# More summed pairs in a feed-forward down product: the first group's and the last 1024 columns'

## The chip, the cores and the metric

The kernel runs on one core of one Trainium2 chip. The metric is the device time of one launch in microseconds (us), the median of several runs. The times of the kernel before come from three runs; one further execution was recorded by the hardware profiler, and all rows of the trace are from that one.

## The reference, cut to what matters

One encoder block on 256 tokens of width 2048 in float32. Two attentions side by side, a cross attention and a gated feed-forward each add to the running sum x, and a last RMSNorm closes it:

```python
x = x + concat([mla(h), diff_attn(h)]) @ w_out      # h = rms_norm(x, g_mix), projected by w_in
x = x + cross_attention(rms_norm(x), rms_norm(mem)) @ w_xo
hf = rms_norm(x, g_ffn)
x = x + (silu(hf @ w_gate) * (hf @ w_up)) @ w_down  # w_gate, w_up: 2048 x 5632; w_down: 5632 x 2048
return rms_norm(x, g_final)
```

The change touches the last product, by `w_down`, and the end of it most of all.

## The kernel before

**Products in three parts.** Every float32 operand is split in two fp32r terms: a high one, which ScalarE (ACT) makes by a cast (line 103), and a low one, which VectorE (DVE) makes as the operand minus its high term (line 104). `mm` then issues three matmuls for one product, with lines of their own: 95 (high by high), 96 (high activation by low weight), 97 (low activation by high weight). A weight block thus passes SyncE's (SP) DMA queue into a `wraw` buffer, ACT into `wh`, DVE into `wl`, and TensorE (PE) last. There are three `wraw` buffers and four each of `wh` and `wl`. The two token halves (tt 0 and 1) are 128 rows each; activations are the stationary operand, 128x128, and weights the moving one, 512 or 256 columns wide. Results gather in eight PSUM banks in two sets of four, which swap their parts after each wide product.

**Plain and summed pairs.** Wide products take the contraction in pairs: 256 rows, two blocks of 128, by 1024 columns, two tiles of 512. A plain pair ("P" in a string of kinds) is 2 blocks x 2 token halves x 2 column tiles = 8 products, 24 matmuls of 512, and its weights take two splits of 128x1024. A summed pair ("W") does the same 2x2x2 block product with seven products instead of eight (a Strassen-Winograd scheme), 21 matmuls. Its weights cost sums ahead of the splits: in `wide_project`, one add of 128x1024 (line 726), two of 128x512 (730 and 731) in a single buffer called `tsum`, and then splits of 1024 (`wh`/`wl`, from the raw block), 1024 (from the sums), 512 (raw) and 1024 (from the sums, in buffers `wh2`/`wl2` of which there is one each). Four of the seven products go into banks of their own, Q 1, 5, 6 and 7, which sum over all summed pairs of one wide product; after the last of these, `leave` (lines 777 to 785 in `wide_add`) adds them to the running sum x in eight DVE steps and one ACT copy, and at the end of the product `join` (788) adds the four plain accumulators. The activation side of a summed pair is made once by `summed_pair` (four 128x128 subtractions, lines 689 to 692, and splits).

**The feed-forward in groups.** The 5632 hidden columns are one narrow chunk of 512 and five wide ones of 1024; a chunk's gate and up products, SiLU (842) and multiply (852) are followed by transposes (858), so that each wide chunk yields four pairs for the down product and the narrow one two. Group 0 is the narrow chunk and one wide chunk: six pairs, kinds `PPPPPW`. Groups 1 and 2 have two wide chunks, eight pairs each, kinds `PPWWPPPW`. Each group multiplies its pairs with their rows of `w_down` and adds the result to x, for columns 0 to 1023 and 1024 to 2047 in turn.

**The end.** In group 2, the first half of the columns is a `wide_add` of all eight pairs. As each of its column tiles is joined, `final` squares it on ACT for the norm (line 199) and multiplies it by `g_final` on GpSimd (POOL, line 893). The second half is done in columns of 512: tile 2 by `project`, four pieces of four plain 128-row blocks, 96 matmuls of 512; then tile 3 as four accumulations of 256 columns (two token halves by two column halves), 192 matmuls of 256. There the first ten blocks are multiplied as they come, and the last six are held split in activation buffers, so that the four accumulations end one after another while the norm of the earlier ones is under way.

**What sets the order.** Each engine runs its instructions in an order that a scheduler fixed when the program was built; only the weight loads on SP keep the order of the code. An engine waits at an instruction until its operands and its buffer are there, and everything queued behind it on the engine waits too.

Of the kernel before, what the change touches and what calls it, by code (L numbers as in the profile page):

```python
# [19 lines left out]
P = 128  # L20
S = 256
NT = S // P
D = 2048
# [16 lines left out]

G_ORDER, U_ORDER = (0, 1, 2, 3, 4, 5, 6, 7), (0, 2, 1, 4, 3, 6, 5, 7)

DN_KINDS = "PP" + "PPPW" + ("PPWW" + "PPPW") * (NPC // 2)

PLAIN, SUMS = ((0, 0), (0, 1), (1, 0), (1, 1)), ((0, 1), (0, 0), (1, 1), (1, 0))
EPS = 1e-6
# [30 lines left out]
def encoder_block(ctx: ExitStack, tc: tile.TileContext, a, out):  # L77
# [15 lines left out]
    def mm(o, l, r, start, stop):  # L93

        nc.tensor.matmul(o, l.h, r.h, start=start, stop=False)  # L95
        nc.tensor.matmul(o, l.h, r.l, start=False, stop=False)  # L96
        nc.tensor.matmul(o, l.l, r.h, start=False, stop=stop)  # L97
# [597 lines left out]
        split_into(f[:, 4:8, :], s)  # L695
        return Pair(forms=f)

    def wide_project(pairs, src, order, kinds, leave, join):

        accs = [[acc_tile() for _ in range(2)] for _ in range(NT)]
        used = [[False] * 2 for _ in range(NT)]
        summed = [i for i in order if kinds[i] == "W"]
        Q = {}  # L710
        for n, i in enumerate(order):
            stop = n == len(order) - 1
            raw = pair_raw(src[i])
# [12 lines left out]
            nc.vector.tensor_tensor(out=t[:, 0:2, :], in0=raw[:, 1:3, :],  # L726
                                    in1=raw[:, 0:1, :].to_broadcast([P, 2, 512]), op=ALU.add)
            t13 = split_blocks(t[:, 0:2, :])
            b21 = split_blocks(raw[:, 3:4, :])
            nc.vector.tensor_tensor(out=t[:, 2, :], in0=t[:, 0, :], in1=raw[:, 2, :], op=ALU.add)  # L730
            nc.vector.tensor_tensor(out=t[:, 3, :], in0=t[:, 2, :], in1=raw[:, 3, :], op=ALU.add)  # L731
# [12 lines left out]
        for tt in range(NT):  # L744
            for oc in range(2):
                join(tt, oc, accs[tt][oc])
        banks.reverse()

    def wide_result(pairs, src, order, kinds):

# [15 lines left out]
        wide_project(pairs, src, order, kinds, leave, join)  # L766
        return res

    def wide_add(pairs, src, order, kinds, oc0, done=None):


        def x(tt, oc):
            return x_res[tt][:, (oc0 + oc) * 512:(oc0 + oc + 1) * 512]

        def leave(Q):
            v, u = nat("v"), nat("u")
            nc.scalar.copy(out=u, in_=Q[1])
            nc.vector.tensor_tensor(out=v, in0=Q[6], in1=u, op=ALU.subtract)
            nc.vector.tensor_tensor(out=x(0, 0), in0=x(0, 0), in1=Q[1], op=ALU.add)
            nc.vector.tensor_tensor(out=u, in0=Q[5], in1=v, op=ALU.add)  # L780
            nc.vector.tensor_tensor(out=v, in0=v, in1=Q[7], op=ALU.subtract)
            nc.vector.tensor_tensor(out=x(1, 1), in0=x(1, 1), in1=Q[5], op=ALU.add)
# [9 lines left out]
        wide_project(pairs, src, order, kinds, leave, join)  # L792

    def normalized_pairs():

# [72 lines left out]
    fss = small.tile([P, NT, 7], F32, name="fss", tag="fss", bufs=1)  # L868
    nc.gpsimd.memset(fss[:, :, 4:5], EPS)

    groups = [([0], (0, 1, 2, 5, 3, 4)), ([1, 2], (0, 1, 2, 4, 3, 6, 7, 5)), ([3, 4], (0, 1, 2, 4, 3, 6, 7, 5))]
    pair0 = 0
    for gi, (chunks, order) in enumerate(groups):
        hp = []
# [20 lines left out]
        def xT(kt):  # L895
            return tuple(hp[kt // 2].at(kt % 2, tt) for tt in range(NT))

        wide_add(hp, src[0], order, kinds, 0, final)
        for oc in (2, 3):
            pieces = [a["w_down"][c, oc - 2] for c in range(len(hp) // 2)]  # L900
            if oc == 2:
                add_out(project(xT, pieces), oc)
                for tt in range(NT):
                    final(tt, oc)
                continue

            accs = [(acc_tile(), ps_tile("acc2")) for _ in range(NT)]
            n = 4 * len(pieces) - 6
            kt = 0
            ws = []  # L910

            def last_mm(tt, h, kt, w, stop):
                mm(accs[tt][h][:, :256], xT(kt)[tt], w[:, h * 256:(h + 1) * 256], kt == 0, stop)
# [10 lines left out]
            for tt in range(NT):  # L924
                for h in range(2):
                    for i, w in enumerate(ws):
                        last_mm(tt, h, n + i, w, i == len(ws) - 1)
                    xs = x_res[tt][:, oc * 512 + h * 256:oc * 512 + (h + 1) * 256]
                    nc.vector.tensor_tensor(out=xs, in0=xs, in1=accs[tt][h][:, :256], op=ALU.add)
                    if h == 0:  # L930
                        meansq(xs, fss[:, tt, 3:4], 256, D)
                        nc.vector.tensor_tensor(out=xs, in0=xs, in1=gfb[1][:, 512:768], op=ALU.mult)
                        nc.vector.reduce_sum(out=fss[:, tt, 5:6], in_=fss[:, tt, 0:5], axis=AX.X)
                        continue
                    sq = nat("sq")[:, :256]
                    nc.vector.tensor_tensor_reduce(out=sq, in0=xs, in1=xs, scale=1.0 / D, scalar=fss[:, tt, 5:6],
                                                   op0=ALU.mult, op1=ALU.add, accum_out=fss[:, tt, 6:7])
                rf = small.tile([P, 1], F32, name="rf", tag="rf")
                nc.gpsimd.tensor_tensor(out=rf, in0=fss[:, tt, 6:7], in1=mhalf[:, :1], op=ALU.pow)
                xr, orow = x_res[tt], out[tt * P:(tt + 1) * P, :]  # L940
                nc.vector.tensor_scalar(out=xr[:, :384], in0=xr[:, :384], scalar1=rf, scalar2=None, op0=ALU.mult)
                nc.sync.dma_start(out=orow[:, :384], in_=xr[:, :384])
                nc.scalar.activation(xr[:, 384:1152], xr[:, 384:1152], AF.Copy, scale=rf)
                nc.scalar.dma_start(out=orow[:, 384:1152], in_=xr[:, 384:1152])
                nc.vector.scalar_tensor_tensor(out=xs, in0=xs, scalar=rf, in1=gfb[1][:, 768:1024],
                                               op0=ALU.mult, op1=ALU.mult)
                nc.vector.tensor_scalar(out=xr[:, 1152:1792], in0=xr[:, 1152:1792], scalar1=rf, scalar2=None,
                                        op0=ALU.mult)
                nc.sync.dma_start(out=orow[:, 1152:], in_=xr[:, 1152:])

# [20 lines left out]
def _lay_out(i):  # L971
# [38 lines left out]
        "w_down": _pieces(i["w_down"][0][-2048:, 1024:]).transpose(1, 0, 2, 3, 4),  # L1010
    }
    return {k: np.ascontiguousarray(v) for k, v in arrays.items()}

# [16 lines left out]
```

## Time and profile before

| | us |
|---|---|
| median of three runs (1147.09 to 1147.89) | 1147.54 |
| the profiled execution | 1148.3 |
| its span, first to last instruction | 1146.5 |
| last matmul starts, from the span's start | 1138.94 |
| mean granted TensorE clock | 0.998 |
| VectorE busy | 944.0 |
| ScalarE busy | 633.8 |

The span is what the instructions cover; 1.8 us of the profiled execution lie outside it. The page gives busy time by engine, the chain of work that ended last, and groups of equal instructions by code line; behind it, the trace answers for one engine and a stretch of time. In a row of the timeline stand the start, the length, the engine, the line, the operation and what it reads and writes; numbers of buffers are left out of the names there.

### The profile page before, as it was taken

How to read it: one execution, taken by the hardware profiler on the slowest of the kernel's cores; microseconds unless marked ns; L12 is line 12 of the kernel's file. 1: busy time of each engine (PE TensorE's matmuls, PEld its weight loads, DVE VectorE, ACT ScalarE, POOL GpSimd, SP SyncE). 2: the span in 40 equal slices, each digit the busy share in tenths (PEclk: the TensorE clock that was granted, in tenths of full speed). 3: DMA queues.
4: the chain of work that ended last, by engine and by line, in shares of the span. 5: the costliest groups of instructions: out<-in, count | busy, mean ns of one | idle time of the engine just before them, and what ended most of it. 6: DMA issues, size and time to landing. Idle time of an engine off the chain costs nothing.

```text
span 1146.5 us, 14402 instructions
## 1 busy us (share of the span) xinstructions
PE 1137.0 (99%) x5471; PEld 954.7 (83%) x5471; DVE 944.0 (82%) x1256; ACT 633.8 (55%) x895; POOL 69.4 (6%) x81
## 2 busy tenths in 40 slices
PE   9999999999999999999999999999999999999997
PEld 7888888888888888888888888888888888888887
DVE  6788766686868677989888888998999898998973
ACT  6755454454566555665544555665554564654652
POOL 4920000000000000000000000000000000000021
PEclk9999999999999999999999999999999999999999
DMA  9655334444854444455555556555555555565561
GB/s 343 234 198 184 143 113 181 163 168 164 313 196 172 150 177 166 169 206 197 210 194 196 194 198 220 183 187 217 184 192 212 206 198 198 192 240 210 189 220 75
DMA packets 33766, 222.15 MB, mean 194 GB/s; under 512 B 4128, under 2 KB 4896, under 8 KB 8992
## 3 DMA queue, kind: packets, MB, share of 16 engines
q1 hardware_dynamic: 32256, 216.86, 52.5%
q0 software_dynamic: 864, 3.15, 0.8%
q10 hardware_dynamic: 576, 1.21, 0.3%
q8 instruction: 43, 0.70, 0.2%
q14 instruction: 27, 0.22, 0.1%
HBM read 219.11 MB, written 2.10 MB: 193 GB/s over the span
## 4 chain that ended last, share of the span: by engine, by line
PE 98%; issue 0%; DMA 0%; DVE 0%; ACT 0%; POOLq 0%; POOL 0%; DVEq 0%; ACTq 0%
PE acc L95 27%; PE acc L97 27%; PE acc L96 27%; PE q L97 3%; PE q L96 3%; PE q L95 3%; PE pt L331 2%; PE ppt L478 1%; PE psc L97 1%; PE psc L96 1%; PE psc L95 1%; PE acckv L95 0%; PE acckv L96 0%; PE acckv L97 0%; PE pt L858 0%
## 5 line engine op out<-in xcount | busy, mean ns | idle before, releaser
L103 ACT CAST wh<-wraw 128x1024 fp32r<-128x1024 f32 (+2 forms) x399 | 392.8, 999 | 353.1 <-PE acc L97 301.6
L104 DVE TENSOR_TENSOR wl<-wraw,wh 128x1024 fp32r<-128x1024 f32 (+2 forms) x399 | 459.9, 1165 | 127.8 <-ACT wh L103 125.9
L96 PE MATMUL acc<-wl,x2n_h 128*128 128x512 f32 x320 | 124.5, 390 | 0.0
L97 PE MATMUL acc<-wh,x2n_l 128*128 128x512 f32 x320 | 123.9, 389 | 0.0
L103 ACT CAST wh<-tsum 128x1024 fp32r<-128x1024 f32 x82 | 85.8, 1051 | 43.9 <-DVE tsum L731 15.1
L104 DVE TENSOR_TENSOR wl<-tsum,wh 128x1024 fp32r<-128x1024 f32 x82 | 99.6, 1220 | 12.5 <-ACT wh L103 12.5
L95 PE MATMUL acc<-wh,x2n_h 128*128 128x512 f32 x320 | 108.1, 390 | 0.0
L96 PE MATMUL acc<-wl,x0T_h 128*128 128x512 f32 x224 | 88.3, 395 | 0.0
L97 PE MATMUL acc<-wh,x0T_l 128*128 128x512 f32 x224 | 88.2, 395 | 0.0
L95 PE MATMUL acc<-wh,x0T_h 128*128 128x512 f32 x224 | 87.3, 395 | 0.8 <-ACT x0T_h L106 0.8
L96 PE MATMUL acc<-wl,hT_h 128*128 128x512 f32 (+1 forms) x192 | 73.0, 383 | 0.0
L97 PE MATMUL acc<-wh,hT_l 128*128 128x512 f32 (+1 forms) x192 | 72.1, 381 | 0.0
L97 PEld LDWEIGHTS acc<-wh,x2n_l 128*128 128x128 f32 x320 | 60.1, 188 | 12.4
L96 PEld LDWEIGHTS acc<-wl,x2n_h 128*128 128x128 f32 x320 | 60.1, 188 | 12.3
L95 PEld LDWEIGHTS acc<-wh,x2n_h 128*128 128x128 f32 x320 | 59.9, 188 | 12.2
L95 PE MATMUL acc<-wh,hT_h 128*128 128x512 f32 (+1 forms) x192 | 64.4, 382 | 0.0
L96 PE MATMUL q<-wl,forms_h 128*128 128x512 f32 x164 | 63.8, 389 | 0.0
L97 PE MATMUL q<-wh,forms_l 128*128 128x512 f32 x164 | 63.5, 389 | 0.0
L95 PE MATMUL q<-wh,forms_h 128*128 128x512 f32 x164 | 57.6, 389 | 0.0
L96 PE MATMUL acc<-wl,forms_h 128*128 128x512 f32 (+1 forms) x151 | 57.0, 378 | 0.0
L97 PE MATMUL acc<-wh,forms_l 128*128 128x512 f32 (+1 forms) x151 | 56.9, 378 | 0.0
L95 PE MATMUL acc<-wh,forms_h 128*128 128x512 f32 (+1 forms) x151 | 56.6, 378 | 0.0
(383 smaller groups left out, 2296.8 us busy)
## 6 DMA issues: line engine op xcount, KB each, us to landing
wraw<-in_w_gate SPq DMA_DIRECT2D x44, 1024.0 KB, 4.8
wraw<-in_w_up SPq DMA_DIRECT2D x44, 1024.0 KB, 4.8
wraw<-in_w_dn SPq DMA_DIRECT2D x36, 1024.0 KB, 4.8
wraw<-in_w_in SPq DMA_DIRECT2D x24, 1024.0 KB, 4.8
wraw<-in_w_out SPq DMA_DIRECT2D x16, 1024.0 KB, 4.8
wraw<-in_w_down SPq DMA_DIRECT2D x8, 1024.0 KB, 4.8
wraw<-in_w_in_lat SPq DMA_DIRECT2D x7, 832.0 KB, 7.7
wraw<-in_w_xk SPq DMA_DIRECT2D x4, 1024.0 KB, 5.7
```

The source lines that it names most:

```text
L95: nc.tensor.matmul(o, l.h, r.h, start=start, stop=False)
L96: nc.tensor.matmul(o, l.h, r.l, start=False, stop=False)
L97: nc.tensor.matmul(o, l.l, r.h, start=False, stop=stop)
L103: last_cast[0] = nc.scalar.copy(out=dst.h, in_=src).ins
L104: last_split[0] = nc.vector.tensor_tensor(out=dst.l, in0=src, in1=dst.h.bitcast(F32), op=ALU.subtract).ins
L331: nc.tensor.transpose(out=pt[:, j * P:(j + 1) * P], in_=src[:, j * P:(j + 1) * P], identity=ident)
L478: nc.tensor.transpose(out=pt[:, kt * S + tt * P:kt * S + (tt + 1) * P], in_=p[:, tt, kt * P:(kt + 1) * P], identity=ident)
```

## The change

Three things are changed.

1. In group 0, the fifth pair (index 4) becomes a summed one: kinds `PPPPWW`, in the order 0, 1, 2, 4, 5, 3. This holds for both halves of the columns.
2. In group 2, the second half of the columns starts with a `wide_add` of five pairs, 0, 2, 3, 7, 1 in this order, with kinds P, W, W, W, P. The Q banks are left as ever; of the plain accumulators only column tile 3's are joined (`closed=(1,)`), and those of tile 2 are handed back open.
3. The remaining pairs 4, 5 and 6, all plain, follow by column tile: 36 matmuls of 512 go on in the open accumulators of tile 2, and then 72 of 256 columns do tile 3 from six weight blocks held in activation buffers, again as four accumulations one after another, which are added to x beside what the five joint pairs gave it. Their weights come in six loads of 512 KB (three of each tile); the second half's `w_dn` pairs come in five loads of 1024 KB. Before, the same 8 MB came in eight loads.

The whole program has 5396 matmuls instead of 5471: 4490 of 512 columns instead of 4445, 504 of 256 instead of 624, the others as before.

```diff
-DN_KINDS = "PP" + "PPPW" + ("PPWW" + "PPPW") * (NPC // 2)
+DN_KINDS = "PP" + "PPWW" + ("PPWW" + "PPPW") * (NPC // 2)
...
-    def wide_project(pairs, src, order, kinds, leave, join):
+    def wide_project(pairs, src, order, kinds, leave, join, closed=(0, 1)):
...
-                            mm(accs[tt][oc], pairs[i].at(k, tt), w[k][:, oc, :], not used[tt][oc], stop and k == 1)
+                            mm(accs[tt][oc], pairs[i].at(k, tt), w[k][:, oc, :], not used[tt][oc],
+                               stop and k == 1 and oc in closed)
...
-            for oc in range(2):
+            for oc in closed:
                 join(tt, oc, accs[tt][oc])
         banks.reverse()
+        return accs
...
-    groups = [([0], (0, 1, 2, 5, 3, 4)), ([1, 2], (0, 1, 2, 4, 3, 6, 7, 5)), ([3, 4], (0, 1, 2, 4, 3, 6, 7, 5))]
+    groups = [([0], (0, 1, 2, 4, 5, 3)), ([1, 2], (0, 1, 2, 4, 3, 6, 7, 5)), ([3, 4], (0, 1, 2, 4, 3, 6, 7, 5))]
...
         wide_add(hp, src[0], order, kinds, 0, final)
-        for oc in (2, 3):
-            pieces = [a["w_down"][c, oc - 2] for c in range(len(hp) // 2)]
-            if oc == 2:
-                add_out(project(xT, pieces), oc)
...
-            for p in pieces:
-                for w in weights(p, pool=act_tile if kt + 4 > n else None):
-                    if kt < n:
-                        for tt in range(NT):
-                            for h in range(2):
-                                last_mm(tt, h, kt, w, False)
-                    else:
-                        ws.append(w)
-                    kt += 1
...
+        accs = wide_add(hp, src[1], (0, 2, 3, 7, 1), kinds, 2, closed=(1,))
+        kts = [2 * i + k for i in (4, 5, 6) for k in range(2)]
+        kt = 0
+        for p in range(3):
+            for w in weights(a["w_down"][0, p]):
                 for tt in range(NT):
-                    final(tt, oc)
-                continue
+                    mm(accs[tt][0], xT(kts[kt])[tt], w, False, kt == 5)
+                kt += 1
+        add_out([accs[tt][0] for tt in range(NT)], 2)
+        for tt in range(NT):
+            final(tt, 2)
+
+        ws = [w for p in range(3) for w in weights(a["w_down"][1, p], pool=act_tile)]
+        oc = 3
+        for tt in range(NT):
+            for h in range(2):
+                acc = acc_tile("acc2")[:, :256]
+                for i, w in enumerate(ws):
+                    mm(acc, xT(kts[i])[tt], w[:, h * 256:(h + 1) * 256], i == 0, i == len(ws) - 1)
```

The rest of the end, the norm and the writes of the output, is the same code. By two or three lines, what stands behind the edits has moved down: the adds are lines 728, 732 and 733 now, `leave` 780 to 788, `join` 791.

VectorE's queue of before at the start of the second column half: the first split of the half's weights is row 1 (`wl_9495`), rows with `v`, `u` and `xres` are the first half's `leave` and `join`.

```order
L104 TENSOR_TENSOR wl_9495<-wraw_9492,wh_9494 128x1024
L778 TENSOR_TENSOR v_9429<-q6_9233,u_9430 128x512
L104 TENSOR_TENSOR wl_9499<-wraw_9492,wh_9498 128x1024
L780 TENSOR_TENSOR u_9430<-q5_9231,v_9429 128x512
L782 TENSOR_TENSOR xres1_109<-xres1_109,q5_9231 128x512
L781 TENSOR_TENSOR v_9429<-v_9429,q7_9232 128x512
L783 TENSOR_TENSOR xres0_108<-xres0_108,u_9430 128x512
L788 TENSOR_TENSOR xres0_108<-xres0_108,acc_9156 128x512
L104 TENSOR_TENSOR wl_9529<-wraw_9526,wh_9528 128x1024
```

The same place of the changed program; `tsum_9561` is the second half's first sum, `wraw_9555` the weights it is made of:

```order
L104 TENSOR_TENSOR wl_9524<-wraw_9521,wh_9523 128x1024
L781 TENSOR_TENSOR v_9456<-q6_9260,u_9457 128x512
L104 TENSOR_TENSOR wl_9528<-wraw_9521,wh_9527 128x1024
L728 TENSOR_TENSOR tsum_9561<-wraw_9555 128x1024
L783 TENSOR_TENSOR u_9457<-q5_9258,v_9456 128x512
L785 TENSOR_TENSOR xres1_109<-xres1_109,q5_9258 128x512
L791 TENSOR_TENSOR xres0_108<-xres0_108,acc_9183 128x512
L732 TENSOR_TENSOR tsum_9561<-tsum_9561,wraw_9555 128x512
L104 TENSOR_TENSOR wl_9563<-wraw_9555,wh_9562 128x1024
L784 TENSOR_TENSOR v_9456<-v_9456,q7_9259 128x512
L786 TENSOR_TENSOR xres0_108<-xres0_108,u_9457 128x512
L104 TENSOR_TENSOR wl_9568<-tsum_9561,wh_9567 128x1024
```

The wide add stands right behind the two plain splits now, and the rest of the sum's work among the first half's `leave` and `join`. VectorE's queue goes on with the end of that first sum and the second pair's (`wraw_9602`, `tsum_9604`):

```order
L733 TENSOR_TENSOR tsum_9561<-tsum_9561,wraw_9555 128x512
L787 TENSOR_TENSOR xres1_109<-xres1_109,v_9456 128x512
L788 TENSOR_TENSOR xres1_109<-xres1_109,v_9456 128x512
L791 TENSOR_TENSOR xres0_108<-xres0_108,acc_9184 128x512
L104 TENSOR_TENSOR wl_9572<-wraw_9555,wh_9571 128x512
L791 TENSOR_TENSOR xres1_109<-xres1_109,acc_9185 128x512
L791 TENSOR_TENSOR xres1_109<-xres1_109,acc_9186 128x512
L104 TENSOR_TENSOR wl2_9578<-tsum_9561,wh2_9577 128x1024
L104 TENSOR_TENSOR wl_9606<-wraw_9602,wh_9605 128x1024
L728 TENSOR_TENSOR tsum_9604<-wraw_9602 128x1024
L732 TENSOR_TENSOR tsum_9604<-tsum_9604,wraw_9602 128x512
L733 TENSOR_TENSOR tsum_9604<-tsum_9604,wraw_9602 128x512
```

From `tsum_9561`'s wide add to `tsum_9604`'s, both counted, stand 6 steps of 1024 and 13 of 512. Behind them come splits of 1024 (`wl_9611`), 512 (`wl_9615`), 1024 (`wl_9649`) and 1024 (`wl2_9621`), the third sum's wide add (`tsum_9647`), two half adds and the split `wl_9654`.

TensorE's queue of the changed program where the second sum is used:

```order
L96 MATMUL q1_9557<-wl_9606,forms_h_8473 128x512
L97 MATMUL q1_9557<-wh_9605,forms_l_8474 128x512
L96 MATMUL acc_9518<-wl_9606,forms_h_8473 128x512
L97 MATMUL acc_9518<-wh_9605,forms_l_8474 128x512
L95 MATMUL q5_9558<-wh_9610,forms_h_8473 128x512
L95 MATMUL q7_9559<-wh_9610,forms_h_8473 128x512
L95 MATMUL acc_9517<-wh_9614,forms_h_8473 128x512
L95 MATMUL q1_9557<-wh_9648,forms_h_9164 128x512
L95 MATMUL acc_9518<-wh_9648,forms_h_9164 128x512
L96 MATMUL q5_9558<-wl_9611,forms_h_8473 128x512
```

The fifth of these rows, the first to read a cast of `tsum_9604`, is the 60th matmul from the first of the second half; the first to read `wh_9653`, the third sum's, is the 81st, and the first to read `wl_9654` the 84th.

More of the change, by code (lines that the diff above doesn't have):

```diff
@@ L767, in wide_result, with wide_add @@
         return res
-    def wide_add(pairs, src, order, kinds, oc0, done=None):
+    def wide_add(pairs, src, order, kinds, oc0, done=None, closed=(0, 1)):
         def x(tt, oc):
@@ L790, in join @@
                 done(tt, oc0 + oc)
-        wide_project(pairs, src, order, kinds, leave, join)
+        return wide_project(pairs, src, order, kinds, leave, join, closed)
     def normalized_pairs():
@@ new lines, in encoder_block @@
+        oc = 3
[4 more added lines that the diff above has]
+                    mm(acc, xT(kts[i])[tt], w[:, h * 256:(h + 1) * 256], i == 0, i == len(ws) - 1)
+                xs = x_res[tt][:, oc * 512 + h * 256:oc * 512 + (h + 1) * 256]
+                nc.vector.tensor_tensor(out=xs, in0=xs, in1=acc, op=ALU.add)
+                if h == 0:
+                    meansq(xs, fss[:, tt, 3:4], 256, D)
+                    nc.vector.tensor_tensor(out=xs, in0=xs, in1=gfb[1][:, 512:768], op=ALU.mult)
+                    nc.vector.reduce_sum(out=fss[:, tt, 5:6], in_=fss[:, tt, 0:5], axis=AX.X)
+                    continue
+                sq = nat("sq")[:, :256]
+                nc.vector.tensor_tensor_reduce(out=sq, in0=xs, in1=xs, scale=1.0 / D, scalar=fss[:, tt, 5:6],
+                                               op0=ALU.mult, op1=ALU.add, accum_out=fss[:, tt, 6:7])
+            rf = small.tile([P, 1], F32, name="rf", tag="rf")
+            nc.gpsimd.tensor_tensor(out=rf, in0=fss[:, tt, 6:7], in1=mhalf[:, :1], op=ALU.pow)
+            xr, orow = x_res[tt], out[tt * P:(tt + 1) * P, :]
+            nc.vector.tensor_scalar(out=xr[:, :384], in0=xr[:, :384], scalar1=rf, scalar2=None, op0=ALU.mult)
+            nc.sync.dma_start(out=orow[:, :384], in_=xr[:, :384])
+            nc.scalar.activation(xr[:, 384:1152], xr[:, 384:1152], AF.Copy, scale=rf)
+            nc.scalar.dma_start(out=orow[:, 384:1152], in_=xr[:, 384:1152])
+            nc.vector.scalar_tensor_tensor(out=xs, in0=xs, scalar=rf, in1=gfb[1][:, 768:1024],
+                                           op0=ALU.mult, op1=ALU.mult)
+            nc.vector.tensor_scalar(out=xr[:, 1152:1792], in0=xr[:, 1152:1792], scalar1=rf, scalar2=None,
+                                    op0=ALU.mult)
+            nc.sync.dma_start(out=orow[:, 1152:], in_=xr[:, 1152:])
@@ L1009, in _lay_out @@
         "w_dn": _pairs(i["w_down"][0], DN_KINDS),
-        "w_down": _pieces(i["w_down"][0][-2048:, 1024:]).transpose(1, 0, 2, 3, 4),
+        "w_down": _pieces(i["w_down"][0][-1024:-256, 1024:], nk=2),
     }
```

32 lines of the change are left out of this document (removed).

## Prediction

> **What bounds the kernel now.** I read the page first, then TensorE's waits, then the stretches around the two edits. The profiled execution took 1148.3 us, 0.8 above the median of the runs (1147.54). Its span, TensorE's row of busy times and the shares of the chain that ended last:
>
> ```profile
> span 1146.5 us, 14402 instructions
> PE 1137.0 (99%) x5471; PEld 954.7 (83%) x5471; DVE 944.0 (82%) x1256; ACT 633.8 (55%) x895; POOL 69.4 (6%) x81
> PE 98%; issue 0%; DMA 0%; DVE 0%; ACT 0%; POOLq 0%; POOL 0%; DVEq 0%; ACTq 0%
> ```
>
> And everything that TensorE waited for:
>
> ```profile
> PE wps L213 <- DVE warm L207: 1.2, 1, 1.2
> PE acc L95 <- ACT x0T_h L106: 0.8, 1, 0.8
> PE po L95 <- ACT val_h L106: 0.2, 1, 0.2
> ```
>
> That is 2.2 us in all, none of it near the edits. So a matmul taken out is worth its pitch, and a stall put in costs its length, with nothing between to swallow either. VectorE (DVE) is the runner-up at 82%, but that is an average, and the question is its load just where it gets more.
>
> **Pitches.** TensorE around the last 1024 columns, single rows of its timeline (start, length of one, a run of adjacent rows counted by x). Pitches come from starts, since neighbours overlap:
>
> ```profile
> 1092.22 0.62 PE L95 MATMUL acc<-wh,hT_h 128*128 128x512 f32 x2
> ...
> 1107.64 0.39 PE L97 MATMUL acc<-wh,hT_l 128*128 128x512 f32 x1
> ...
> 1110.36 0.39 PE L97 MATMUL acc<-wh,hT_l 128*128 128x512 f32 x1
> ...
> 1116.03 0.28 PE L95 MATMUL acc<-wh,hT_h 128*128 128x256 f32 x1
> ...
> 1127.54 0.28 PE L95 MATMUL acc<-w_h,hT_h 128*128 128x256 f32 x1
> ...
> 1138.94 0.28 PE L97 MATMUL acc<-w_h,forms_l 128*128 128x256 f32 x1
> ```
>
> The rows at 1107.64 and 1110.36 are 12 matmuls apart: 2.72/12 = 0.2267 us for 512 columns. Those at 1116.03 and 1127.54 are 96 apart: 0.120 us for 256. The first matmul of the second column half is the second one of the top row, at 1092.45. From there before issues 104 matmuls of 512 (8 of them left over from the first half) and 192 of 256.
>
> VectorE's prices, two stretches of its timeline:
>
> ```profile
> 1079.86 1.22 DVE L726 TENSOR_TENSOR tsum<-wraw 128x1024 f32<-128x1024 f32 x1
> 1081.12 0.69 DVE L730 TENSOR_TENSOR tsum<-tsum,wraw 128x512 f32<-128x512 f32 x1
> 1081.84 0.69 DVE L731 TENSOR_TENSOR tsum<-tsum,wraw 128x512 f32<-128x512 f32 x1
> 1082.45 1.22 DVE L104 TENSOR_TENSOR wl<-tsum,wh 128x1024 fp32r<-128x1024 f32 x1
> ...
> 1086.54 3.49 DVE L104 TENSOR_TENSOR wl<-wraw,wh 128x1024 fp32r<-128x1024 f32 x3
> ...
> 1091.68 0.68 DVE L780 TENSOR_TENSOR u<-q,v 128x512 f32<-128x512 f32 x1
> 1092.28 0.68 DVE L782 TENSOR_TENSOR xres<-xres,q 128x512 f32<-128x512 f32 x1
> ```
>
> A 1024-wide step has a pitch of (3.49-1.22)/2 = 1.14 us, a 512-wide one 0.60 (1091.68 to 1092.28). The result is there about 0.08 after the pitch. Where one add reads what the last wrote, that shows: the three adds of a sum start 1.26, 0.72 and 0.61 apart, 2.59 together.
>
> **Edit 1, group 0: one plain pair becomes summed, in both column halves.** TensorE saves 2 x 3 matmuls of 512: 6 x 0.2267 = 1.36 us. VectorE: a plain pair is two wide splits, 2.28 us; a summed one three wide splits, one wide add, two half adds and a half split, 4 x 1.14 + 3 x 0.60 = 6.36. That is 4.1 more per half. The activation side of the new pair costs four 128x128 subtractions and a 512-wide split more; the group of one of the four, of seven such pairs:
>
> ```profile
> L690 DVE TENSOR_TENSOR sums<-pt,sums 128x128 f32<-128x128 f32 x7 | 2.0, 284 | 0.0
> ```
>
> At 0.284 less the 0.08 of overlap that is 4 x 0.20 + 0.60 = 1.4, and 2 x 4.1 + 1.4 = 9.6 us in all. Room for it, by stretches of 15 us around group 0's down product (engine busy, count, ..., clock):
>
> ```profile
> 560.00:575.00 15.00, 15.00 (x74) 12.51 (x73) 13.90 (x19) 7.06 (x9) 0.00 (x0) 1.00 0.45 172
> 575.00:590.00 15.00, 15.00 (x70) 12.40 (x69) 11.75 (x19) 9.01 (x13) 0.00 (x0) 1.00 0.41 141
> 590.00:605.00 15.00, 15.00 (x68) 12.42 (x67) 14.54 (x18) 5.96 (x6) 0.00 (x0) 1.00 0.69 227
> 605.00:620.00 15.00, 15.00 (x68) 12.40 (x67) 10.29 (x12) 7.75 (x10) 0.00 (x0) 1.00 0.52 193
> ```
>
> VectorE is idle for 1.1 + 3.25 + 0.46 + 4.71 = 9.5 us there, so the addition just fits, and TensorE runs some way behind the splits. I take no wait. If the cover is gone, the worst I can build is the new pair's own activation work in the open, 1.4 us.
>
> **Edit 2, the last 1024 columns: work.** After issues 155 matmuls of 512 (the same 8 among them) and 72 of 256. Before: 96 x 0.2267 + 192 x 0.120 = 44.80 us without the 8; after: 147 x 0.2267 + 72 x 0.120 = 41.97. Saved: 2.84 us. With edit 1, 4.20.
>
> **Edit 2: waits.** Three summed pairs now stand in a row. They cost VectorE 3 x 6.36 = 19.1 us and TensorE 3 x 21 x 0.2267 = 14.3 us, and the first begins while VectorE still empties the first half's sums. So I go through the queue in the order of the changed program. VectorE reaches the add that forms the first sum at 1091.68, where before has its first 512-wide step after two splits. From there through the second sum's wide add stand 6 wide and 13 half steps: 6 x 1.14 + 13 x 0.60 = 14.64, so it ends at 1106.32, its result is there at 1106.40, and ScalarE (ACT) must cast it. The length of that cast:
>
> ```profile
> 1084.31 1.05 ACT L103 CAST wh<-tsum 128x1024 fp32r<-128x1024 f32 x1 [0.28 <-DVE xres L779]
> ```
>
> Cast done at 1107.45. The matmul that needs it, the second pair's first of q5, is the 60th from 1092.45: TensorE is there at 1092.45 + 59 x 0.2267 = 1105.82. **Wait 1: 1.63 us.** Everything behind it on TensorE, plain pairs too, waits with it.
>
> The second sum's adds start at 1105.18 and take 2.59, to 1107.77. Then come three wide splits and a half one (3.42 + 0.60), to 1111.79. There is one buffer for the sums, so the third wide add cannot start before the last of these splits is through: 1113.01, result at 1113.09, cast at 1114.14. The 81st matmul needs it; TensorE would be there at 1107.45 + 21 x 0.2267 = 1112.21. **Wait 2: 1.93 us.** Behind it two half adds and a wide split put the low term at 1115.43; the 84th matmul would want it at 1114.82. **Wait 3: 0.61 us.** Together 4.17. After that VectorE has only plain splits, and those of the six last pieces are done in time: six loads of 512 KB instead of two of 1024, each 3.3 to 4.8 us, queued long before. TensorE's end by this ledger: 1115.43 + 72 x 0.2267 + 72 x 0.120 = 1140.39 against 1138.94 + 0.12 = 1139.06 before: +1.33, which is 4.17 - 2.84. What follows the last matmul is the same chain in both.
>
> **Edit 2: GpSimd's multiplies beside VectorE.** The final multiplies of columns 0 to 1023 run on GpSimd (POOL) in this stretch. Before, these splits fell beside them:
>
> ```profile
> 1096.45 1.81 POOL L893 TENSOR_TENSOR xres<-xres,gfb 128x512 f32<-128x512 f32 x1 [74.52 <-ACT junk L199]
> 1098.98 1.51 POOL L893 TENSOR_TENSOR xres<-xres,gfb 128x512 f32<-128x512 f32 x1 [0.72 <-ACT junk L199]
> 1101.66 4.56 POOL L893 TENSOR_TENSOR xres<-xres,gfb 128x512 f32<-128x512 f32 x2 [1.16 <-ACT junk L199]
> ...
> 1097.61 1.73 DVE L104 TENSOR_TENSOR wl<-wraw,wh 128x1024 fp32r<-128x1024 f32 x1
> ...
> 1103.71 1.34 DVE L104 TENSOR_TENSOR wl<-wraw,wh 128x1024 fp32r<-128x1024 f32 x1 [0.91 <-ACT wh L103]
> ```
>
> Against 1.22 elsewhere they took 0.51 and 0.12 more: 0.6 us over four multiplies. In before this was covered; now VectorE is what TensorE waits for, so it lands on the path. I take 0.6; the bounds are 0 and four times the longer, 2.04. The Trainium skill ("SBUF — State Buffer", section "Who interferes with whom") says that a two-input VectorE instruction and a GpSimd one that reads SBUF share a port, which the first to issue holds for its whole length. The rows agree that there is a hold-up, but a much shorter one than a whole multiply.
>
> **Sum.** -1.36 - 2.84 + 4.17 + 0.6 = +0.57 us: 1148.9 for the profiled execution, and 1147.54 + 0.57 = **1148.1 us** as the median.
>
> **Rivals.** A measurement of this kernel tells apart about 0.2%, 2.3 us: 1145.25 and 1149.83 are the edges.
>
> A: *the waits do not come.* For it: before shows TensorE with no wait at all in this stretch, with much VectorE work, and VectorE there has idle time:
>
> ```profile
> 1093.00:1116.00 23.00, 23.00 (x103) 19.05 (x102) 17.27 (x19) 13.40 (x19) 7.88 (x4) 1.00 0.56 204
> ```
>
> 5.7 of 23 us. Against it: that idle time lies behind 1100, and the queue above has none. It gives -4.20: 1143.3. Chance 0.10. Were the ledger half wrong, -4.20 + 2.09: 1145.4.
>
> B: *slower: GpSimd's multiplies lock VectorE out for their whole length.* Place: the 14.64 us before wait 1, full of two-input steps. Price: four times about 1.5 us (the single row at 1098.98) instead of 0.6: -4.20 + 4.17 + 6.0, 1153.5. It decides from 2.3 us in total, about 0.58 per multiply. Against: the two rows at 0.51 and 0.12. For: in the changed order VectorE never pauses there, so every multiply meets it. Chance 0.12. This is also what the skill's rule would make of it.
>
> C: *group 0 has no cover:* +1.4, 1149.5, still within 0.2%. Chance 0.08.
>
> D: *the change does not do what it says:* excluded, the changed order holds 5396 matmuls instead of 5471, in the places named.
>
> **How the numbers follow.** The forecast itself gets 0.70. The range reaches from the half-wrong ledger, 1145.4, to the upper price of the multiplies with 0.2 us of error on each of three waits: -4.20 + 4.17 + 2.04 + 0.6 = +2.6, 1150.2. Outside lie A and B, 0.22 less what of B stays small: about 0.2. Faster by over 0.2% is A and a sliver: 0.11. Slower is B and the top of the range: 0.14. Same: 0.75.
>
> **What would show it.** TensorE's waits in the changed profile should list three on a high term cast or low term split from the sums, 1.6, 1.9 and 0.6 us, all within 1105 to 1116, and none in 550 to 620. The first matmul of the second half should come about 1.4 us earlier than 1092.45, and the last about 0.6 later than 1138.94. VectorE should show no idle time from there to wait 3. I am wrong if TensorE runs through (A), if the splits beside the multiplies take 2.5 us or more (B), or if a wait appears on a load or a PSUM bank, which I have at nothing.

## The result, and the profile after

The changed kernel takes **1154.67 us** (median of six runs, 1153.61 to 1155.78); the kernel before, on the same chip, 1147.41. The ratio is 1.0064, 95% interval 1.0051 to 1.0077: **7.3 us slower**, where 0.6 was forecast. The profiled execution took 1154.45 us. Its span, TensorE's busy row and the shares of the chain:

```profile
span 1152.7 us, 14322 instructions
PE 1137.1 (99%) x5396; PEld 948.6 (82%) x5396; DVE 972.6 (84%) x1296; ACT 641.2 (56%) x908; POOL 66.2 (6%) x81
PE 93%; DVE 4%; DMA 1%; ACT 1%; issue 1%; SPq 0%; POOLq 0%; POOL 0%; DVEq 0%; ACTq 0%
```

TensorE has 75 matmuls less and yet the same busy time, 1137.1 against 1137.0 us: some of its matmuls must have become longer. VectorE has come onto the chain. What TensorE waited for, the first five rows:

```profile
PE q L95 <- ACT wh L103: 2.4, 2, 2.2
PE q L96 <- DVE wl L104: 2.4, 3, 1.0
PE wps L213 <- DVE warm L207: 1.2, 1, 1.2
PE acc L95 <- ACT x0T_h L106: 0.4, 1, 0.4
PE acc L95 <- ACT wh L103: 0.4, 1, 0.4
```

The first two, 4.8 us, lie in the last half, on casts and splits as foreseen, though two of the five come at the 52nd and the 56th matmul of the half, where the ledger (the prediction's account of VectorE's queue, step by step) had none. But the span grew by 6.15 us, so waits are not the whole story. By the starts of matmuls in the two traces:

| | before | after | difference |
|---|---|---|---|
| first matmul of the second column half | 1092.45 | 1090.70 | -1.75 |
| its matmuls at 0.2267 and 0.120 us | 46.61 | 43.78 | -2.84 |
| what TensorE loses between them | 0.0 | 9.51 | +9.51 |
| from the last matmul's start to the end of the span | 7.58 | 8.79 | +1.21 |

Forecast for the third row were 4.77 (4.17 of waits and 0.6 for the multiplies), for the fourth nothing. The loss of 9.51 us, in VectorE's timeline: the first sum's wide add, the steps that were longer than their kind, and the step behind them.

```profile
1089.93 1.22 DVE L728 TENSOR_TENSOR tsum<-wraw 128x1024 f32<-128x1024 f32 x1
...
1095.19 1.39 DVE L786 TENSOR_TENSOR xres<-xres,u 128x512 f32<-128x512 f32 x1
1096.50 1.21 DVE L104 TENSOR_TENSOR wl<-tsum,wh 128x1024 fp32r<-128x1024 f32 x1
...
1101.84 1.92 DVE L104 TENSOR_TENSOR wl<-tsum,wh 128x1024 fp32r<-128x1024 f32 x1
1103.68 2.31 DVE L104 TENSOR_TENSOR wl<-wraw,wh 128x1024 fp32r<-128x1024 f32 x1
1105.91 2.31 DVE L728 TENSOR_TENSOR tsum<-wraw 128x1024 f32<-128x1024 f32 x1
1108.26 0.69 DVE L732 TENSOR_TENSOR tsum<-tsum,wraw 128x512 f32<-128x512 f32 x1
```

And GpSimd's multiplies at the same time, and the two of column tile 2 at the end:

```profile
1094.74 1.29 POOL L896 TENSOR_TENSOR xres<-xres,gfb 128x512 f32<-128x512 f32 x1 [74.56 <-ACT junk L199]
1101.38 5.77 POOL L896 TENSOR_TENSOR xres<-xres,gfb 128x512 f32<-128x512 f32 x3 [5.34 <-ACT junk L199]
1140.01 2.84 POOL L896 TENSOR_TENSOR xres<-xres,gfb 128x512 f32<-128x512 f32 x2 [32.87 <-ACT junk L199]
```

Each of the four long steps stands beside a multiply. From start to start: 1.31 instead of 0.60, 1.84 and 2.23 instead of 1.14, 2.35 instead of 1.26 (an add whose result the next step reads). That is 0.71 + 0.70 + 1.09 + 1.09 = **3.6 us**, not 0.6. All other steps between have the pitches of the prediction.

The second part shows in TensorE's own timeline:

```profile
1103.81 0.50 PE L96 MATMUL q<-wl,forms_h 128*128 128x512 f32 x1 [0.85 <-DVE wl L104]
...
1106.04 0.50 PE L96 MATMUL q<-wl,forms_h 128*128 128x512 f32 x1 [1.04 <-DVE wl L104]
...
1106.84 0.39 PE L97 MATMUL acc<-wh,forms_l 128*128 128x512 f32 x1
1109.41 1.22 PE L95 MATMUL q<-wh,forms_h 128*128 128x512 f32 x2 [2.17 <-ACT wh L103]
...
1111.90 0.63 PE L96 MATMUL q<-wl,forms_h 128*128 128x512 f32 x1
1112.32 0.63 PE L97 MATMUL q<-wh,forms_l 128*128 128x512 f32 x1
```

After the wait of 2.17 us the matmuls come 0.427 us apart instead of 0.2267. The granted clock says why; it is the third number from the end of each row, ahead of the DMA share and GB/s:

```profile
1104.61:1108.03 3.42, 1.58 (x6) 0.67 (x4) 3.42 (x2) 0.00 (x0) 2.53 (x2) 1.00 0.05 22
1108.03:1114.85 6.82, 5.44 (x12) 3.97 (x13) 6.72 (x8) 3.46 (x4) 0.00 (x0) 0.50 0.23 78
1114.85:1118.00 3.15, 2.89 (x13) 1.93 (x11) 1.70 (x4) 2.23 (x4) 0.00 (x0) 1.00 0.00 0
```

Half the clock for 6.8 us, with 12 matmuls in it that cost 2.75 us more than their pitch. So of the 9.51 us: 5.33 up to the 60th matmul (it starts 18.71 us behind the first of the half instead of 13.38), which is the ledger's first wait of 1.63 and the 3.6 of the multiplies but for 0.1; 2.75 at half clock; and 1.4 in the two short waits after it, with the 0.1 us or so that comes behind each wait (at full clock the first pitch after one is 0.33 us).

### The profile page after: what moved, and what is told of

It reads as the page before. It is cut to its first block, busy times and chain, and to the rows that moved or that the text cites. A ratio compares the mean times of both kernels' runs of the same rounds, so it can differ in the third digit from the quotient of the medians.

```text
span 1152.7 us, 14322 instructions
## 1 busy us (share of the span) xinstructions
PE 1137.1 (99%) x5396; PEld 948.6 (82%) x5396; DVE 972.6 (84%) x1296; ACT 641.2 (56%) x908; POOL 66.2 (6%) x81
## 3 DMA queue, kind: packets, MB, share of 16 engines
q10 hardware_dynamic: 576, 1.21, 0.3%
## 4 chain that ended last, share of the span: by engine, by line
PE 93%; DVE 4%; DMA 1%; ACT 1%; issue 1%; SPq 0%; POOLq 0%; POOL 0%; DVEq 0%; ACTq 0%
PE acc L95 25%; PE acc L96 25%; PE acc L97 25%; PE q L95 3%; PE q L97 3%; PE q L96 3%; DVE wl L104 2%; PE pt L331 2%; DMA wraw<-in_w_down 1%; PE ppt L478 1%; PE psc L97 1%; PE psc L96 1%; PE psc L95 1%; DMA wraw<-in_w_in_lat 0%; DVE tsum L728 0%
## 5 line engine op out<-in xcount | busy, mean ns | idle before, releaser
L103 ACT CAST wh<-tsum 128x1024 fp32r<-128x1024 f32 x92 | 96.5, 1050 | 49.4 <-DVE tsum L728 19.9
L104 DVE TENSOR_TENSOR wl<-tsum,wh 128x1024 fp32r<-128x1024 f32 x92 | 112.6, 1226 | 12.3 <-ACT wh L103 12.3
L96 PE MATMUL q<-wl,forms_h 128*128 128x512 f32 x184 | 72.4, 393 | 2.4 <-DVE wl L104 2.4
L97 PE MATMUL q<-wh,forms_l 128*128 128x512 f32 x184 | 71.9, 392 | 0.0
L96 PE MATMUL acc<-wl,hT_h 128*128 128x512 f32 x184 | 71.7, 392 | 0.0
L97 PE MATMUL acc<-wh,hT_l 128*128 128x512 f32 x184 | 70.8, 389 | 0.0
L97 PEld LDWEIGHTS acc<-wh,x2n_l 128*128 128x128 f32 x320 | 60.1, 188 | 12.5
L95 PE MATMUL acc<-wh,hT_h 128*128 128x512 f32 x184 | 63.8, 391 | 0.0
L728 DVE TENSOR_TENSOR tsum<-wraw 128x1024 f32<-128x1024 f32 x46 | 57.1, 1241 | 1.3 <-DMA wraw<-in_w_dn 0.7
L95 PE MATMUL acc<-wh,forms_h 128*128 128x512 f32 x138 | 54.2, 394 | 0.1
L96 PE MATMUL acc<-wl,forms_h 128*128 128x512 f32 x138 | 53.9, 391 | 0.0
```

What stands on the lines that cost most here:

```text
L103: last_cast[0] = nc.scalar.copy(out=dst.h, in_=src).ins
L104: last_split[0] = nc.vector.tensor_tensor(out=dst.l, in0=src, in1=dst.h.bitcast(F32), op=ALU.subtract).ins
```

## The experiments

**1. Group 0 alone.** The kernel before with the first of the three edits:

```diff
-DN_KINDS = "PP" + "PPPW" + ("PPWW" + "PPPW") * (NPC // 2)
+DN_KINDS = "PP" + "PPWW" + ("PPWW" + "PPPW") * (NPC // 2)
...
-    groups = [([0], (0, 1, 2, 5, 3, 4)), ...
+    groups = [([0], (0, 1, 2, 4, 5, 3)), ...
```

> The kernel before with the change in group 0 alone: six pairs of kinds PPPPWW, the last 1024 columns as before. Theory: six matmuls of 512 go, 6 x 0.2267 = 1.36 us, VectorE's extra work is hidden, nothing else moves: 1147.4 - 1.4 = 1146.0 us, no wait of TensorE between 540 and 625. Rival (group 0 without cover): up to 1.4 us back, 1147.4, with a wait of TensorE in that stretch.

Measured: 1146.6 us against 1147.6, ratio 0.9988 (0.9979 to 0.9997). No wait of TensorE between 500 and 640. Two of the stretches shown before, now:

```profile
575.00:590.00 15.00, 15.00 (x69) 12.40 (x68) 14.09 (x26) 9.21 (x16) 0.00 (x0) 1.00 0.40 141
605.00:620.00 15.00, 15.00 (x68) 12.43 (x67) 14.17 (x17) 8.54 (x10) 0.00 (x0) 1.00 0.44 157
```

VectorE went from 11.75 and 10.29 to 14.09 and 14.17 us of 15, TensorE kept its 15.00. The step holds: 1.0 us won by the medians, 1.4 by the ratio, and all the loss is at the end of the kernel.

**2. Without the four early multiplies** (left out of the computation), all other queues the same:

```diff
             meansq(xs, fss[:, tt, oc:oc + 1], 512, D)
+            if oc < 2:
+                return
             nc.gpsimd.tensor_tensor(out=xs, in0=xs, in1=gfb[...], op=ALU.mult)
```

> The changed kernel without the four multiplies by g_final on GpSimd for columns 0 to 1023 (left out of the computation); the order of all other engines is the same. Theory: four VectorE steps beside these multiplies took 0.71, 0.70, 1.09 and 1.10 us longer than elsewhere, 3.6 us, before the second sum, so the first three waits (0.85, 1.04 and 2.17 us) shrink to about the 1.6 us of the ledger, the granted clock stays at 1.00 there, the later two waits grow as TensorE is no longer held back: in all 1154.7 less 3.6 to 5.5, 1149 to 1151. Rival (VectorE is simply slower in this order than its pitches, the multiplies only happen to stand beside): the steps keep their lengths, within 1 us of 1154.7. Rival (the clock alone is to blame, it falls whenever TensorE stands for about 2 us): steps shorter, but the clock still falls to 0.5 for some 6.8 us and two thirds of the gain is lost, 1152 to 1153.

Measured: 1149.37 us, ratio 1.0012 (1.0003 to 1.0022): some 5 us of the 7.3 are gone. VectorE around the second sum's wide add:

```profile
1101.20 1.22 DVE L104 TENSOR_TENSOR wl<-tsum,wh 128x1024 fp32r<-128x1024 f32 x1
1102.34 1.22 DVE L104 TENSOR_TENSOR wl<-wraw,wh 128x1024 fp32r<-128x1024 f32 x1
1103.47 1.22 DVE L728 TENSOR_TENSOR tsum<-wraw 128x1024 f32<-128x1024 f32 x1
1104.72 0.69 DVE L732 TENSOR_TENSOR tsum<-tsum,wraw 128x512 f32<-128x512 f32 x1
```

The same three steps that took 1.92, 2.31 and 2.31 are 1.22 each. From the first sum's wide add (1090.00) to the end of this one, 1103.47 + 1.14, are 14.61 us; the ledger had 14.64. The rival that VectorE is slower in this order by itself falls. Of the waits 1.5 us remain within 3.4, and in this profiled execution (1150.99 us) the clock fell once more, for one such stretch:

```profile
1104.56:1107.97 3.41, 1.89 (x8) 1.02 (x7) 3.34 (x6) 3.19 (x4) 0.00 (x0) 1.00 0.01 2
1107.97:1111.38 3.41, 3.41 (x10) 2.65 (x9) 3.38 (x3) 0.27 (x1) 0.00 (x0) 0.50 0.45 154
```

**3. The multiplies held back.** Nothing is left out; GpSimd multiplies the four pieces only when the third sum is formed:

```diff
...
+            zero = small.tile([P, 1], F32, name="zero", tag="zero", bufs=1)
+            nc.gpsimd.tensor_scalar(out=zero, in0=col, scalar1=0.0, scalar2=None, op0=ALU.mult)
+            for oc in range(2):
+                g = gfb[0][:, oc * 512:oc * 512 + 1]
+                nc.gpsimd.tensor_tensor(out=g, in0=g, in1=zero, op=ALU.add)
...
```

> The changed kernel with the same four multiplies held back until the third sum is formed (the gain row gets 0 times one of its values added, so that GpSimd has to wait for it); nothing is left out. Theory: as without them, 1149 to 1151, since VectorE has spare time once the summed pairs are through; at most 1 us more, where they meet the last splits. Rival (a multiply costs VectorE the same wherever it stands): near 1154.

Measured: 1154.8 us, as the rival said, ratio 1.0062 (1.0048 to 1.0075), but not for the rival's reason. TensorE's waits in the last half were only 2.3 us and its clock stayed up. The time had been lost before: from about 500 on the matmuls came on average about 1% further apart, the 2700th to the 5000th in 519.3 us instead of 514.2. The suspicion was the new tile of 4 bytes. Two runs settle it.

**4. The same with no new tile**, the zero in a column that is written later anyway:

```diff
-            zero = small.tile([P, 1], F32, name="zero", tag="zero", bufs=1)
+            zero = fss[:, 1, 6:7]
```

> The changed kernel with the four multiplies held back until the third sum is formed, as in the run with the late multiplies, but without its new tile of 4 bytes a partition: the zero stands in a column of the table of squares that is written later anyway. In that earlier run TensorE's waits after 1085 were as short as without the multiplies, but from about 540 on every 512-column matmul came about 1% further apart (0.2290 us instead of 0.2267), 5 us by 1054. Theory: that was the new tile, which moves all that is allocated behind it by 4 bytes; now the time is that of the run without the multiplies, 1149.4, up to 1 us more. Rival (holding the multiplies back costs 5 us in some other way): 1154.8 again.

Measured: 1149.5 us, ratio 1.0014 (1.0005 to 1.0023), the time of experiment 2 with nothing left out. In this profiled execution the first waits (at the 60th and the 63rd matmul) were those of experiment 2, and the clock did not fall:

```profile
1103.42:1106.83 3.41, 1.89 (x8) 1.21 (x8) 3.38 (x5) 3.41 (x4) 0.00 (x0) 1.00 0.01 2
1106.83:1110.24 3.41, 3.41 (x16) 2.57 (x14) 3.38 (x4) 0.80 (x3) 0.00 (x0) 1.00 0.46 154
```

With neither multiplies nor half clock in the way, the ledger can be read against it: the 81st matmul starts 21.77 us behind the first of the half (ledger 21.69), the 84th 23.03 (22.98), the last ends at 48.21 (47.94).

**5. Four bytes alone.** The kernel before with one unused tile, set once and never read:

```diff
+    four = small.tile([P, 1], F32, name="four", tag="four", bufs=1)
+    nc.gpsimd.memset(four, 0.0)
     fss = small.tile([P, NT, 7], F32, name="fss", tag="fss", bufs=1)
```

> The kernel before with one more tile of 4 bytes a partition, set to zero once at the start and never read; the order on all other engines is the same. Theory: that shift of all later tiles is what cost the run with the late multiplies 5 us, so this one takes about 1152.6, with the 512-column matmuls 0.2290 us apart from 540 on. Rival (something else in that run): 1147.6.

Measured: 1153.82 us, ratio 1.0054 (1.004 to 1.0068). The stretch from 620 to 1090 in this kernel, and then in the kernel before:

```profile
620.00:1090.00 470.00, 470.00 (x2086) 385.70 (x2085) 430.24 (x510) 258.25 (x304) 1.10 (x2) 1.00 0.56 199
```

```profile
620.00:1090.00 470.00, 470.00 (x2107) 389.58 (x2106) 433.09 (x514) 262.48 (x308) 1.10 (x2) 1.00 0.56 202
```

Both busy throughout at full clock, but 21 matmuls fewer fit into the 470 us.

**6. Spaced.** The changed kernel with pair 1 between the first two summed pairs:

```diff
-        accs = wide_add(hp, src[1], (0, 2, 3, 7, 1), kinds, 2, closed=(1,))
-        kts = [2 * i + k for i in (4, 5, 6) for k in range(2)]
+        accs = wide_add(hp, src[1], (0, 2, 1, 3, 7, 4), kinds, 2, closed=(1,))
+        kts = [2 * i + k for i in (5, 6) for k in range(2)]
...
```

> The changed kernel with the last half's joint pairs in another order and one more of them: plain, summed, plain, summed, summed, plain, then only the last two pairs by column tile. One plain pair between the first and the second summed pair gives VectorE 24 matmuls, 5.4 us, of TensorE's time for 2.3 us of its own. Theory: the first waits shrink by the difference, 3.1 us, and the clock holds; the two summed pairs that stay in a row still make TensorE wait about 2 us: 1154.7 - 3.1 - 2.5, about 1149; 1147 to 1151. Rival (the multiplies take whatever is given): over 1152.

Measured: 1151.65 us, ratio 1.0033 (1.002 to 1.0045): between the two expectations. The wait at the second summed pair was gone, a later wait of 2.1 us and half clock behind it (3.4 us) remained. Here GpSimd paid far more: three multiplies in a row took 13.83 us. The first of them was held through nine VectorE steps that followed each other without a pause:

```profile
1102.15 9.37 POOL L896 TENSOR_TENSOR xres<-xres,gfb 128x512 f32<-128x512 f32 x1 [6.29 <-ACT junk L199]
```

VectorE paid as well: the steps beside the four multiplies were 0.7 to 1.1 us longer, as in the changed kernel.

**7. Without any of the six multiplies** (left out of the computation):

```diff
-            nc.gpsimd.tensor_tensor(out=xs, in0=xs, in1=gfb[...], op=ALU.mult)
```

> The changed kernel without any of the six multiplies of 512 columns by g_final on GpSimd (left out of the computation): beside the four early ones also the two of column tile 2, which stand in the last 10 us. Behind the last matmul the changed kernel takes 8.8 us, the kernel before 7.6, and a VectorE step of the end took 1.34 or 1.59 us beside these two instead of 0.48. Theory: their hold-up, about 1.1 us, is on the path at the end: 1149.4 less 1.1, about 1148.3, and 7.6 to 8.0 us behind the last matmul. Rival (the end is longer because column tile 2 is joined so late that its squares keep ScalarE from the last ones): 1149.4 and about 9 us.

Measured: 1148.18 us, ratio 1.0004 (0.9995 to 1.0013), 1.2 less than in experiment 2. From the last matmul (1139.29) to the end of the span (1146.69) are 7.40 us instead of 9.14 there. The two late multiplies are what lengthened the end. In the changed kernel:

```profile
1141.79 1.34 DVE L930 CUSTOM_DVE_ANT_0 sq<-xres,fss 128x256 f32<-128x256 f32 x1
```

The same step took 0.48 in the kernel before, where tile 2 had been done 20 us earlier.

**8. Woven**, column tile 2's pairs among the summed ones, and **9. woven, multiplies late**:

```diff
-        accs = wide_add(hp, src[1], (0, 2, 3, 7, 1), kinds, 2, closed=(1,))
+        accs = wide_add(hp, src[1], (0, 2, tile2(0), 3, tile2(1), tile2(2), 7, 1), kinds, 2, closed=(0, 1), done=closing)
...
```

Here `tile2(p)` stands for the 12 matmuls of pair 4 + p in column tile 2; in 9 the call also gets `split_done=late_mult`, the multiplies held back as in experiment 4.

> The changed kernel with column tile 2's three plain pairs put between the summed ones: pair 0, summed 2, tile 2 of pair 4, summed 3, tile 2 of pairs 5 and 6, summed 7, pair 1, and at the end the 72 matmuls of 256 for tile 3. Same matmuls, same weights, multiplies where they were. Each tile-2 pair gives VectorE 12 matmuls, 2.7 us, of TensorE's time for 1.1 us of its own. Theory: with the multiplies still in the way before the second sum, 3.6 us, the first waits shrink by 1.6 and the later ones go: 1149 to 1151. Rival (the multiplies alone are to blame, spacing is worth nothing): 1154. Rival (spacing alone is enough): below 1146.

> As the woven order, and the four multiplies held back until the last joint pair's weights are split. Nothing is left out. Theory: the ledger holds (14.6 us from the first sum's wide add to the second's), so TensorE waits at most 0.5 us in the last half, the clock stays at 1.00, and all of the 4.20 us of matmuls is kept but for that and up to 1 us at the end: 1143.5 to 1145. Rival (another limit shows once this one is gone, loads or PSUM banks): 1146 or more, with a wait of TensorE on it.

Measured: 1151.48 us, ratio 1.0032 (1.0019 to 1.0044), for the woven order, and 1149.51, 1.0013 (1.0004 to 1.0022), with the multiplies late. In the first, one wait of 3.4 us on a split took the place of three, since the multiplies now met the second sum's half adds, and TensorE then ran at half clock for 6.8 us. In the second TensorE lost only 1.2 us in the last half and its last matmul started at 1136.32, 2.6 us ahead of the kernel before: up to there the theory holds. But behind it stood 12.5 us. VectorE was still emptying the second half's sums, beside the multiplies that had been moved there:

```profile
1131.51 1.79 DVE L791 TENSOR_TENSOR xres<-xres,u 128x512 f32<-128x512 f32 x1
1133.22 1.78 DVE L792 TENSOR_TENSOR xres<-xres,v 128x512 f32<-128x512 f32 x1
1134.92 0.68 DVE L793 TENSOR_TENSOR xres<-xres,v 128x512 f32<-128x512 f32 x1
```

The gain was given back at the end; the rival was right about the time, but not with its wait of TensorE.

**10. Two summed pairs, spread.** Pair 3 is plain in the second half (its weights are laid out so), and the plain work comes first:

```diff
-        accs = wide_add(hp, src[1], (0, 2, 3, 7, 1), kinds, 2, closed=(1,))
+        accs = wide_add(hp, src[1], (0, 3, tile2(0), 2, tile2(1), 7, tile2(2), 1), kinds[:3] + "P" + kinds[4:], 2,
+                        closed=(0, 1), done=closing)
...
```

> Two summed pairs in the second half instead of three (pair 3 is plain there), and VectorE's load spread: pairs 0 and 3 plain, tile 2 of pair 4, summed 2, tile 2 of pair 5, summed 7, tile 2 of pair 6, pair 1, then the 72 matmuls of 256. Group 0 as in the changed kernel, the six multiplies where they were. TensorE does three matmuls of 512 more than the changed kernel, 0.68 us; VectorE 4.1 us less. Theory: 60 matmuls, 13.6 us, come before the first summed pair now, which is room for what VectorE has left of the first half (about 6 us), the splits and the 3.6 us of the multiplies; no wait over 0.5 us, the clock stays at 1.00, column tile 2 is done 8.6 us ahead of the end, so that its multiplies meet less of the end: 1147.6 - 1.36 - 2.16 = 1144.1, up to 1 us more. Rival (the summed pairs cost TensorE waits wherever they stand in the last half): 1146.5 or more, with waits on casts or splits of the sums. Rival (the end, behind the last matmul, eats it, as in the woven order with late multiplies, 12.5 us there): no waits, but over 9 us behind the last matmul.

Measured: **1145.52 us** against 1147.65, ratio 0.998 (0.9971 to 0.9989): faster than both kernels, by little. TensorE's waits, all of them, and the stretch in which the kernel before had VectorE busy for 17.27 of 23 us:

```profile
PE wps L213 <- DVE warm L207: 1.2, 1, 1.2
PE acc L95 <- ACT x0T_h L106: 0.6, 1, 0.6
PE po L95 <- ACT val_h L106: 0.2, 1, 0.2
```

```profile
1093.00:1116.00 23.00, 22.91 (x102) 18.64 (x101) 22.96 (x23) 13.46 (x21) 7.42 (x4) 1.00 0.42 152
```

VectorE works without a pause (22.96 of 23), still has four steps lengthened by the multiplies, and TensorE does not wait, since 60 matmuls lie ahead of the first sum. What follows the last matmul takes 8.7 us instead of 7.6, which is most of the difference between 1145.5 and the expected 1144.1. By the traces the second half's matmuls take 1.75 us less than before and the end 1.16 more, so some 0.6 us are won here and the rest is mostly group 0's; the interval overlaps that of experiment 1, so the runs alone do not show that this half wins anything.

## Why the prediction was wrong

**What held.** Group 0: -1.36 forecast; -1.0 by the medians, interval -2.4 to -0.3; no wait. The matmuls of the end: -2.84, as the table has it. The ledger of VectorE's queue: 14.64 us against 14.61, and, once the multiplies were out of the way (experiment 4), the loss up to each of its three places to within 0.2 us. One more wait came in between, at the 63rd matmul, without adding to the sum.

**The step that failed is the price of GpSimd's multiplies**, "I take 0.6; the bounds are 0 and four times the longer, 2.04". It is 3.6 us. The prediction took what two splits of before were longer by, 0.51 and 0.12, for the price of a meeting. Read by their ends, the same rows say more. The multiply at 1096.45 ended at 1098.26; the split issued at 1097.61 ended at 1099.34, which is 1.08 later and nearly its whole pitch of 1.14. The split at 1103.71 ended at 1105.05, again 1.08 behind the end of a multiply (1103.97). Both had stood until the multiply was through, and the excess was only what was left of it when they came. The third early multiply of before by itself, and then the last three of the changed kernel:

```profile
1101.66 2.31 POOL L893 TENSOR_TENSOR xres<-xres,gfb 128x512 f32<-128x512 f32 x1 [1.16 <-ACT junk L199]
```

```profile
1101.38 1.30 POOL L896 TENSOR_TENSOR xres<-xres,gfb 128x512 f32<-128x512 f32 x1 [5.34 <-ACT junk L199]
1102.63 2.28 POOL L896 TENSOR_TENSOR xres<-xres,gfb 128x512 f32<-128x512 f32 x1
1104.87 2.27 POOL L896 TENSOR_TENSOR xres<-xres,gfb 128x512 f32<-128x512 f32 x1
```

Those three end at 1102.68, 1104.91 and 1107.14, and the long VectorE steps beside them at 1103.76, 1105.99 and 1108.22: each 1.08 behind its multiply. The second and third multiply in turn took 2.3 us instead of 1.3, as they waited for the VectorE step before them. So the two engines took turns, each for a whole instruction. VectorE did not pause any more, so its steps came earlier in each multiply and lost 0.70 to 1.09 us every time. If the most that a step can lose to a multiply is its 1.29 us, the upper bound for four, an estimate from these rows, is 5.2 us and not 2.04.

The prediction's remark that the rows show a much shorter hold-up than a whole multiply is thus a misreading: the rows of both traces fit a hold that lasts to the end of the multiply. The Trainium skill ("SBUF — State Buffer", section "Who interferes with whom") says that the order of issue decides which of the two is blocked; the two traces agree with that, as the same multiplies cost VectorE 0.6 in one order and 3.6 in the other. GpSimd's own loss does not tell what VectorE will lose: its four multiplies took 2.7 us more than four of 1.29 in before and 1.9 more in the changed kernel. Rival B, given 0.12, was the mechanism; its price of 6.0 was too high, and that its total came close was luck, because of two other losses that no part of the prediction had.

**The clock.** The prediction priced every wait at its length. In the changed kernel the waits of 0.85, 1.04 and 2.17 us came within 6.5 us, TensorE then ran at half clock for 6.8 us, and 12 matmuls took 2.75 us longer. Part of that would have been waiting anyhow: in experiment 4, with no half clock, the later waits were longer by 0.3 us than in the changed kernel. The Trainium skill ("TensorE: Matmul & The Clock Gate", Part 1) has the clock fall to half after an idle window of about 3.4 us. The half rate agrees; the condition does not, if idle means without matmuls: the longest single wait was 2.2 us, and TensorE had been busy for 1.58 of the 3.42 us ahead of the fall. In experiments 2 and 7 it fell after 1.9 busy of 3.4, in experiment 4 it did not after the same 1.89. Where the border lies, and whether busy time alone decides, was not settled.

**The end.** "What follows the last matmul is the same chain in both" failed by 1.21 us. The chain has the same steps, but column tile 2, which used to be finished 20 us ahead, was finished in it, with its two multiplies beside VectorE's last steps. Experiment 7 takes them away and has 7.40 us there.

Sum, for the profiled span: -1.75 - 2.84 + 9.51 + 1.21 = +6.13, measured 6.15. The first term holds 0.4 us that the start of the kernel gave: the wait on `x0T_h` was 0.4 instead of 0.8, which also varies between runs of kernels that do not differ there. The four early multiplies with what follows from them account for about 5 of the 7.3 us (experiments 2 and 4), the two late ones for about 1.2 (experiment 7). Without all six the kernel takes 0.3 us more than the one before (1.0004, interval 0.9995 to 1.0013); the prediction's other terms come to -0.03.

## What to carry to other kernels

When a row is longer than its kind beside another engine's, compare the ends and not only the lengths. If the held step ends one usual length behind the other engine's instruction, it stood until that one was through, and its excess is only what happened to be left. A change that makes the held engine busier lets it come earlier, so the whole of the other instruction is the bound for the price. And several waits close together can cost more than their lengths, so look at the granted clock behind them.

## What the runs showed of the hardware that was not expected

A tile of 4 bytes a partition that nothing reads slowed the kernel before by 6.2 us (1153.82 against 1147.65), through a mean pitch of TensorE's 512-column matmuls that grew from 0.227 to 0.230 us from about 500 us on, at full clock and with no wait; more than half of them kept 0.227, the others took up to 0.236. The order of all instructions but one memset was the same; the tile shifts what is allocated behind it. Which tile has to lie where was not tried.

VectorE steps that read PSUM kept their length beside a multiply (line 784, 0.60 from start to start, around GpSimd's 1094.74, which itself took its 1.29), while those of the changed kernel with both operands in SBUF did not. In the changed kernel multiplies and such steps took turns; in experiment 6 one multiply was held through nine of them. What decides between the two was not tried.
